# Compression products of a hybrid attention layer: split float32r weights against plain float32 in four column strips

## The chip, the cores and the metric

The kernel runs on one core of a Trainium2 chip. Its time is the device time of one execution in microseconds (us). Before the change it was timed three times, and the median is what a later time is compared with.

## The reference, cut to what matters

One transformer layer over 256 tokens of width 2048, in float32: three attention branches (fox, nsa, dsa), a gated mix, a feed-forward network of width 5632 and a gated extra input. The change touches one piece of the nsa branch: keys and values are compressed. Windows of 32 tokens with a stride of 16 (15 windows) are flattened to 4096 numbers and sent through a two-layer network, once for keys and once for values:

```python
n_cmp = (S - CMP_LEN) // CMP_STRIDE + 1          # 15
tok = c_start[:, None] + jnp.arange(CMP_LEN)[None, :]

def compress(raw, pe, w1, w2):
    blk = (raw[:, tok] + pe).reshape(B, n_cmp, CMP_LEN * dh)   # [15, 32*128]
    return jax.nn.gelu(blk @ w1) @ w2                           # w1 is [4096, 256], w2 is [256, 128]

k_cmp = rope1(compress(kc_raw, pe_k, wk1, wk2), cos[c_end], sin[c_end])
v_cmp = compress(vc_raw, pe_v, wv1, wv2)
```

Only `blk @ w1` is computed in another way after the change. It is 2 x 32 products of a [128 x 15] block with a [128 x 256] piece of `w1`, which is 4 MB for each of the two compressions.

## The kernel before, in words

**Large products.** Nearly all of the time goes to products of the 256 tokens with weight matrices. Each is made of three float32r products: both operands are split into a high and a low half, and high x high, low x high and high x low are summed in PSUM (lines 212 to 214). `weight_group` (line 147) brings one weight tile of 512 KB: a DMA on the queue of SyncE (SP) into `raw` (3 buffers), ScalarE (ACT) rounds it to `whi`, VectorE (DVE) subtracts to get `wlo` (4 buffers each, lines 144 and 145). TensorE (PE) then uses it for 12 products of 512 columns. We call one such tile with its products a stage. A chunk of 512 columns of the input projection has 8 stages, with two accumulators, one for each half of the tokens.

**Side work.** Attention is cut into generators. After every stage `tick()` advances up to three of them, so that their instructions stand between two stages in each engine's program. The tile framework then lays out each engine's instructions by its own plan; the engines work in that order.

**A compression** (`compress`, line 661) is such a generator. `blocks` (line 580) adds the position code to the windows and splits the sum into two halves, side by side in 30 columns. In each of 8 ticks one tile of `w1` (4 of the 32 positions) goes through `weight_group`, with the `raw`, `whi` and `wlo` buffers of the large products, and PE makes 4 x 2 products of 256 columns (lines 670 and 671) with the block as the stationary operand: 30 columns of the array, into 30 rows of one PSUM bank. We call these 8 products a visit; there are 8 visits in a compression, 16 in all. At the end the two halves' rows are summed by a small product with a constant (line 678).

**Neighbours that matter here.** `index_scores` (line 622) makes products for two heads that lie in rows 0 to 63 and 64 to 127 (lines 630 and 631, plain float32). `after_c1` (line 516) normalizes part of the first chunk on DVE (line 530); PE transposes its result at line 537. `queries` and `key_queries` apply rotary tables to a finished chunk with ten DVE instructions (lines 435 to 439), and PE transposes these (lines 446 and 615). `g_tile` (line 342) hands out three buffers of 512 KB, which are used for gates from 330 us on.

Of the kernel before, what the change touches and what calls it, by code (L numbers as in the profile page):

```python
# [10 lines left out]
F32 = mybir.dt.float32  # L11
F32R = mybir.dt.float32r
AF = mybir.ActivationFunctionType
ALU = mybir.AluOpType

P = 128
# [18 lines left out]
NCMP = 15  # L35
# [38 lines left out]
def _const_array():  # L74
    parts, at = [], 0

    def add(name, a):
        nonlocal at
        full = np.zeros((P, a.shape[1]), np.float32)
        full[: a.shape[0]] = a  # L80
        CONST[name] = (at, a.shape[1])
        at += a.shape[1]
        parts.append(full)

    i = np.arange(P)
    causal = np.where(i[None, :] <= i[:, None], 0.0, NEG).astype(np.float32)

    def tables(dim):
        inv = np.float32(1.0) / (np.float32(10000.0) ** (np.arange(0, dim, 2, dtype=np.float32) / np.float32(dim)))
        ang = np.arange(S, dtype=np.float32)[:, None] * inv[None, :].astype(np.float32)  # L90
        return np.cos(ang).astype(np.float32), np.sin(ang).astype(np.float32)

    c, s = tables(HD)
    ci, si = tables(64)
    add("ident", np.eye(P, dtype=np.float32))
    for h in range(2):
        add(f"icos{h}", np.concatenate([ci[h * P:(h + 1) * P]] * 2, 1))
        add(f"isin{h}", si[h * P:(h + 1) * P])
    add("tri", (i[:, None] <= i[None, :]).astype(np.float32))
    CONST["first"] = (0, at)  # L100
    for h in range(2):
        add(f"cos{h}", np.concatenate([c[h * P:(h + 1) * P]] * 2, 1))
        add(f"sin{h}", s[h * P:(h + 1) * P])
    CONST["second"] = (0, at)
    add("mask", np.concatenate([causal, np.zeros((P, P), np.float32), causal], 1))
    ends = np.arange(NCMP) * 16 + 31
    add("cosc", np.concatenate([c[ends]] * 2, 1))
    add("sinc", s[ends])
    ok = (ends[None, :] <= np.arange(S)[:, None]).astype(np.float32)
    for h in range(2):  # L110
        add(f"cmask{h}", np.where(ok[h * P:(h + 1) * P] > 0, 0.0, NEG).astype(np.float32))
    for h in range(2):
        add(f"cok{h}", ok[h * P:(h + 1) * P])
    add("two", np.concatenate([np.eye(NCMP, dtype=np.float32)] * 2, 0))
    return np.concatenate(parts, 1)


# [4 lines left out]
def build(ctx: ExitStack, tc: tile.TileContext, A: dict):  # L122
    nc = tc.nc
    PE, DVE, ACT, POOL = nc.tensor, nc.vector, nc.scalar, nc.gpsimd
# [13 lines left out]
    def sc_tile():  # L138
        return scp.tile([P, 512], F32, name="sc")


    def halves(src, hi, lo):

        ACT.activation(hi, src, AF.Copy)  # L144
        DVE.tensor_sub(lo, src, hi.bitcast(F32))  # L145

    def weight_group(src, nk, w, pool=None):
        raw = wp.tile([P, 1024], F32, name="raw", bufs=3)
        if pool is None:
            hi = wp.tile([P, 1024], F32R, name="whi")  # L150
            lo = wp.tile([P, 1024], F32R, name="wlo")
        else:
            hi, lo = (pool.tile([P, 1024], F32R, name=f"w{x}4", tag="k4") for x in "hl")
        n = nk * w
        nc.sync.dma_start(raw[:, :n].rearrange("p (k w) -> p k w", k=nk), src)
        halves(raw[:, :n], hi[:, :n], lo[:, :n])
        v = lambda t: t[:, :n].rearrange("p (k w) -> p k w", k=nk)
        return v(hi), v(lo)
# [5 lines left out]
    def add(gen, *after):  # L164
        task = {"gen": gen, "after": after, "done": False, "at": 0}
        side.append(task)
        return task
# [174 lines left out]
    def g_tile():  # L342
        return gp.tile([P, 2, 512], F32, name="g", tag="g")
# [10 lines left out]
    with ExitStack() as at:  # L354
        ka = at.enter_context(tc.tile_pool(name="ka", bufs=7))
        cp = at.enter_context(tc.tile_pool(name="cp", bufs=1))
        tm = at.enter_context(tc.tile_pool(name="tm", bufs=2))
# [30 lines left out]
        C = {n: cst[:, a:a + w] for n, (a, w) in CONST.items()}  # L388
        gkv = cp.tile([P, 256], F32, name="gkv")
        fbias = cp.tile([P, 6], F32, name="fbias")  # L390
        peT = cp.tile([P, 2, 32], F32, name="peT")
# [35 lines left out]
        def rope(src, nh, d, cos, sin, out):  # L427

            n = src.shape[0]
            h = d // 2  # L430
            tb = tm.tile([P, 512], F32, name="rb", bufs=1)
            s3 = src.rearrange("p (n d) -> p n d", n=nh)
            o3 = out.rearrange("p (n d) -> p n d", n=nh)
            b3 = tb[:n, :nh * d].rearrange("p (n d) -> p n d", n=nh)
            DVE.tensor_tensor(o3, s3, bc_heads(cos, nh), op=ALU.mult)
            DVE.tensor_tensor(b3[:, :, :h], s3[:, :, h:], bc_heads(sin, nh), op=ALU.mult)
            DVE.tensor_tensor(b3[:, :, h:], s3[:, :, :h], bc_heads(sin, nh), op=ALU.mult)
            DVE.tensor_sub(o3[:, :, :h], o3[:, :, :h], b3[:, :, :h])
            DVE.tensor_add(o3[:, :, h:], o3[:, :, h:], b3[:, :, h:])
# [66 lines left out]
        blk = [None, None]  # L506
        R = {}

        def ra():
            return tm.tile([P, 512], F32, name="ra", bufs=4)  # L510

        def rc():
            return tm.tile([P, P], F32, name="rc")
# [66 lines left out]
        def blocks(j):  # L580

            raw = nsT[:, 2 + j, :]
            win = bass.AP(tensor=raw.tensor, offset=raw.offset, ap=[list(raw.ap[0]), [1, 32], [16, NCMP]])
            a = ra()[:, :32 * NCMP].rearrange("p (l c) -> p l c", l=32)
            DVE.tensor_tensor(a, win, peT[:, j, :].unsqueeze(2).broadcast_to([P, 32, NCMP]), op=ALU.add)
            b = ka.tile([P, 32, 2 * NCMP], F32R, name=f"blk{j}", tag="ka")
            halves(a, b[:, :, :NCMP], b[:, :, NCMP:])
            blk[j] = b


# [69 lines left out]

        def compress(j):
            blocks(j)
            yield
            ph = sc_tile()
            for g in range(8):
                hi, lo = weight_group(A["cmp1"][j, :, g * 4:(g + 1) * 4, :], 4, 256)
                for l in range(4):
                    b = blk[j][:, g * 4 + l, :]
                    first, last = g == 0 and l == 0, g == 7 and l == 3
                    PE.matmul(ph[:2 * NCMP, :256], b, hi[:, l, :], start=first, stop=False)  # L670
                    PE.matmul(ph[:2 * NCMP, :256], b, lo[:, l, :], start=False, stop=last)
                yield
            hid = tm.tile([2 * NCMP, 256], F32, name="hid", bufs=1)
            ACT.copy(hid, ph[:2 * NCMP, :256])
            yield
            pg = sc_tile()
            for n in range(2):
                PE.matmul(pg[:, n * 16:n * 16 + NCMP], hid[:, n * P:(n + 1) * P], C["two"][:2 * NCMP, :],
                          start=True, stop=True)
            x = sm.tile([P, 2, NCMP], F32, name="gx")  # L680
            u = sm.tile([P, 2, NCMP], F32, name="gu")
            DVE.tensor_copy(x, pg[:, :32].rearrange("p (n c) -> p n c", n=2)[:, :, :NCMP])
            DVE.tensor_mul(u, x, x)
            DVE.tensor_mul(u, u, x)
            DVE.scalar_tensor_tensor(u, u, 0.044715, x, op0=ALU.mult, op1=ALU.add)
            ACT.activation(u, u, AF.Tanh, scale=math.sqrt(2.0 / math.pi))
            DVE.tensor_scalar(u, u, 1.0, 0.5, op0=ALU.add, op1=ALU.mult)
            DVE.tensor_mul(u, u, x)
            yield
            pv = sc_tile()  # L690
            for n in range(2):
                PE.matmul(pv[:NCMP, :P], u[:, n, :], cmp2[:, j, n, :], start=(n == 0), stop=(n == 1))
            if j == 1:
                DVE.tensor_copy(cmpv, pv[:NCMP, :P])
                return
            t = rc()
            rope(pv[:NCMP, :P], 1, P, C["cosc"][:NCMP, :], C["sinc"][:NCMP, :], t[:NCMP, :P])
            yield
            tp = sc_tile()
            PE.transpose(tp[:, :NCMP], t[:NCMP, :P], ident[:NCMP, :NCMP])  # L700
            DVE.tensor_copy(cmpk, tp[:, :NCMP])
# [127 lines left out]
    for n in range(4):  # L829
        G = gates(n) if n else G0  # L830
        mix = None
        for name, kt, k0 in (("dsa", 6, 10), ("nsa", 4, 0), ("fox", 6, 4)):
            ps = gemm(A["br_" + name][n], lambda k: O(k0 + k), kt, 512)
            g = G[name]
# [103 lines left out]
    def first_chunk():  # L938
        g = g_tile()
        ps = gemm(A["ffn_in"][0], hT, KT, 512, sizes=[[2] * LONG3], spare=[k4b] * (LONG3 - 4))  # L940
        for h in range(2):
            ACT.activation(g[:, h, :], ps[h], AF.Silu)
        ps = gemm(A["ffn_in"][11], hT, KT, 512)
        for h in range(2):
            DVE.tensor_mul(g[:, h, :], g[:, h, :], ps[h])
        return [g[:, h, :] for h in range(2)]
# [29 lines left out]
    g = first_chunk()  # L976
# [24 lines left out]
    for n in range(4):  # L1001
# [7 lines left out]
        w = 512 // (len(ps) - 1)  # L1009
# [53 lines left out]
```

## Time and profile before

| | us |
|---|---|
| median of three runs | 1613.66 |
| lowest and highest | 1611.16, 1614.71 |
| the profiled execution | 1614.24 |
| its span on the core | 1612.0 |
| PE busy in the span | 1598.5 (99%) |
| DVE busy | 1035.2 (64%) |
| ACT busy | 768.6 (48%) |
| DMA | 198 GB/s over the span |

The span runs from the first to the last instruction of the program. A PE row of the timeline gives the start of a product and the time to its modelled end; since products are pipelined, what one costs is the distance to the next start. `x4` says that four records were merged into one row. PEclk is the granted clock of PE as a share of full speed.

### The profile page before, as it was taken

What the parts mean: (1) busy time and instruction counts of PE and PEld (TensorE: products, weight loads), DVE (VectorE), ACT (ScalarE), POOL (GpSimd) and SP (SyncE); (2) the same over time, 40 slices, a digit from 0 to 9 for tenths busy, and PEclk for the clock granted to TensorE, in tenths of its full rate; (3) what the DMA queues carried; (4) which work ended last, traced back from release to release, by engine and by line L of the source; (5) the groups of instructions that cost most, each with busy time, mean ns of one, the idle gap of its engine ahead of it and who ended that gap; (6) DMA issues with size and microseconds to landing.
All of it is one profiled execution on the core that took longest, in us unless ns stands there. A gap on an engine that the chain in (4) does not pass through costs nothing. (4 is left out here: it accounts for less than half of the span.)

```text
span 1612.0 us, 19950 instructions
## 1 busy us (share of the span) xinstructions
PE 1598.5 (99%) x7521; PEld 1338.9 (83%) x7521; DVE 1035.2 (64%) x1346; ACT 768.6 (48%) x958; POOL 16.9 (1%) x38
## 2 busy tenths in 40 slices
PE   9999999999999999999999999999999999999998
PEld 7777899998888888888888888888888888888787
DVE  5679775554646455465877777787878664545764
ACT  5455554554444444444454444455555453433443
POOL 0000000010000000000000000000000000000000
PEclk9999999999999999999999999999999999999999
DMA  8564654567666666677475565656666776666474
GB/s 266 182 193 148 209 156 117 163 196 237 189 195 186 193 187 193 194 229 222 150 248 170 203 218 200 216 202 222 222 206 223 248 258 194 195 192 199 147 234 132
DMA packets 92752, 319.71 MB, mean 198 GB/s; under 512 B 10608, under 2 KB 11760, under 8 KB 92656
## 3 DMA queue, kind: packets, MB, share of 16 engines
q1 hardware_dynamic: 91376, 314.25, 61.6%
q0 software_dynamic: 1280, 4.20, 0.9%
q8 instruction: 59, 0.97, 0.2%
q14 instruction: 37, 0.30, 0.1%
HBM read 311.58 MB, written 6.82 MB: 198 GB/s over the span
## 5 line engine op out<-in xcount | busy, mean ns | idle before, releaser
L145 DVE TENSOR_TENSOR wlo<-raw,whi 128x1024 fp32r<-128x1024 f32 (+2 forms) x532 | 632.9, 1193 | 498.7 <-ACT whi L144 490.7
L144 ACT ACTIVATE whi<-raw 128x1024 fp32r<-128x1024 f32 (+2 forms) x532 | 549.2, 1035 | 690.1 <-PE acc L213 400.9
L212 PE MATMUL acc<-whi,k4h 128*128 128x512 f32 (+3 forms) x1580 | 608.1, 385 | 1.2 <-ACT k4h L144 0.7
L214 PE MATMUL acc<-wlo,k4h 128*128 128x512 f32 (+3 forms) x1580 | 601.4, 381 | 2.1 <-DVE wlo L145 2.1
L213 PE MATMUL acc<-whi,k4l 128*128 128x512 f32 (+3 forms) x1580 | 602.1, 381 | 0.8 <-DVE k4l L145 0.8
L212 PEld LDWEIGHTS acc<-whi,k4h 128*128 128x128 f32 x1580 | 297.3, 188 | 55.4 <-issue 2.2
L214 PEld LDWEIGHTS acc<-wlo,k4h 128*128 128x128 f32 x1580 | 297.3, 188 | 54.6 <-DVE wlo L145 3.1
L213 PEld LDWEIGHTS acc<-whi,k4l 128*128 128x128 f32 x1580 | 297.6, 188 | 52.1 <-DVE k4l L145 2.0
L257 PE MATMUL sc<-whi,k4h 128*128 128x512 f32 x240 | 94.0, 391 | 0.0
L257 PE MATMUL acc<-whi,k4h 128*128 128x512 f32 x240 | 93.9, 391 | 0.0
L259 PE MATMUL sc<-wlo,k4h 128*128 128x512 f32 x240 | 93.6, 390 | 0.0
L259 PE MATMUL acc<-wlo,k4h 128*128 128x512 f32 x240 | 93.5, 390 | 0.0
L258 PE MATMUL acc<-whi,k4l 128*128 128x512 f32 x240 | 93.5, 390 | 0.0
L258 PE MATMUL sc<-whi,k4l 128*128 128x512 f32 x240 | 93.5, 390 | 0.0
L259 PEld LDWEIGHTS sc<-wlo,k4h 128*128 128x128 f32 x240 | 45.1, 188 | 9.4
L259 PEld LDWEIGHTS acc<-wlo,k4h 128*128 128x128 f32 x240 | 45.1, 188 | 9.4
L258 PEld LDWEIGHTS acc<-whi,k4l 128*128 128x128 f32 x240 | 45.1, 188 | 9.2
L258 PEld LDWEIGHTS sc<-whi,k4l 128*128 128x128 f32 x240 | 45.1, 188 | 9.2
L257 PEld LDWEIGHTS acc<-whi,k4h 128*128 128x128 f32 x240 | 45.1, 188 | 9.2
L257 PEld LDWEIGHTS sc<-whi,k4h 128*128 128x128 f32 x240 | 45.1, 188 | 9.2
L145 DVE TENSOR_TENSOR wtlo<-raw,wthi 128x1024 fp32r<-128x1024 f32 x40 | 48.1, 1223 | 0.0
L144 ACT ACTIVATE wthi<-raw 128x1024 fp32r<-128x1024 f32 x40 | 41.1, 1050 | 1.8 <-DVE raw L282 1.5
(305 smaller groups left out, 1211.9 us busy)
## 6 DMA issues: line engine op xcount, KB each, us to landing
raw<-ffn_in SPq DMA_DIRECT2D x176, 512.0 KB, 4.5
raw<-gate SPq DMA_DIRECT2D x96, 512.0 KB, 3.6
raw<-ffn_out SPq DMA_DIRECT2D x88, 512.0 KB, 4.4
raw<-att_c SPq DMA_DIRECT2D x40, 512.0 KB, 4.4
raw<-att_f SPq DMA_DIRECT2D x48, 384.0 KB, 3.3
raw<-w_out SPq DMA_DIRECT2D x32, 512.0 KB, 4.0
raw<-ple_gate SPq DMA_DIRECT2D x32, 512.0 KB, 4.1
raw<-cmp SPq DMA_DIRECT2D x16, 512.0 KB, 4.4
```

What stands on the lines that cost most here:

```text
L144: ACT.activation(hi, src, AF.Copy)
L145: DVE.tensor_sub(lo, src, hi.bitcast(F32))
L212: PE.matmul(o, xh[:, c], h, start=(k == 0), stop=False)
L213: PE.matmul(o, xl[:, c], h, start=False, stop=False)
L214: PE.matmul(o, xh[:, c], l, start=False, stop=(k == kt - 1))
L257: PE.matmul(o, xh, h, start=first, stop=False)
L258: PE.matmul(o, xl, h, start=False, stop=False)
L259: PE.matmul(o, xh, l, start=False, stop=stop)
```

## The change

The block is no longer split: it is one float32 tile of 32 columns for each position, of which 15 hold windows and 17 are set to zero by GpSimd (POOL). The tiles of `w1` are no longer split either: they are loaded straight into the three `g_tile` buffers and used as they are. A visit now has two tiles: one tick issues their two loads, and the next makes the eight products, each in plain float32 of 256 columns. The four positions of a tile go to four strips of 32 columns of the array (`tile_position=(0, 32 * l)`), and their sums gather in four groups of 32 rows of the PSUM bank. There are 4 visits in a compression, and 8 in all. The constant at the end sums four groups in place of two. A compression still takes 8 ticks for this part.

```diff
-    add("two", np.concatenate([np.eye(NCMP, dtype=np.float32)] * 2, 0))
+    add("four", np.concatenate([np.eye(32, NCMP, dtype=np.float32)] * 4, 0))
...
-            a = ra()[:, :32 * NCMP].rearrange("p (l c) -> p l c", l=32)
-            DVE.tensor_tensor(a, win, peT[:, j, :].unsqueeze(2).broadcast_to([P, 32, NCMP]), op=ALU.add)
-            b = ka.tile([P, 32, 2 * NCMP], F32R, name=f"blk{j}", tag="ka")
-            halves(a, b[:, :, :NCMP], b[:, :, NCMP:])
+            b = ka.tile([P, 32, 32], F32, name=f"blk{j}", tag="ka")
+            POOL.memset(b[:, :, NCMP:], 0.0)
+            DVE.tensor_tensor(b[:, :, :NCMP], win, peT[:, j, :].unsqueeze(2).broadcast_to([P, 32, NCMP]), op=ALU.add)
             blk[j] = b
...
-            for g in range(8):
-                hi, lo = weight_group(A["cmp1"][j, :, g * 4:(g + 1) * 4, :], 4, 256)
-                for l in range(4):
-                    b = blk[j][:, g * 4 + l, :]
-                    first, last = g == 0 and l == 0, g == 7 and l == 3
-                    PE.matmul(ph[:2 * NCMP, :256], b, hi[:, l, :], start=first, stop=False)
-                    PE.matmul(ph[:2 * NCMP, :256], b, lo[:, l, :], start=False, stop=last)
+            for g in range(0, 8, 2):
+                ws = []
+                for i in range(2):
+                    w = g_tile().rearrange("p a (b n) -> p (a b) n", n=256)
+                    nc.sync.dma_start(w, A["cmp1"][j, :, (g + i) * 4:(g + i + 1) * 4, :])
+                    ws.append(w)
                 yield
-            hid = tm.tile([2 * NCMP, 256], F32, name="hid", bufs=1)
-            ACT.copy(hid, ph[:2 * NCMP, :256])
+
+                for i in range(2):
+                    for l in range(4):
+                        PE.matmul(ph[32 * l:32 * (l + 1), :256], blk[j][:, (g + i) * 4 + l, :], ws[i][:, l, :],
+                                  start=(g + i == 0), stop=(g + i == 7), tile_position=(0, 32 * l))
+                yield
+            hid = tm.tile([P, 256], F32, name="hid", bufs=1)
+            ACT.copy(hid, ph[:, :256])
```

The instructions also move against each other, since the framework plans anew. Three places matter. The first is DVE's program at about 37 to 42 us, where the second chunk's weights are split and `after_c1` scales its accumulators (line 530). Before:

```order
L562 SCALAR_TENSOR_TENSOR lf<-lf 128x12
L145 TENSOR_TENSOR wlo<-raw,whi 128x1024 x2
L530 SCALAR_TENSOR_TENSOR ra<-acc,rms,gkv 128x256 x2
L145 TENSOR_TENSOR wlo<-raw,whi 128x1024
L540 COPY nsT<-sc 128x128
```

After:

```order
L562 SCALAR_TENSOR_TENSOR lf<-lf 128x12
L145 TENSOR_TENSOR wlo<-raw,whi 128x1024
L530 SCALAR_TENSOR_TENSOR ra<-acc,rms,gkv 128x256 x2
L145 TENSOR_TENSOR wlo<-raw,whi 128x1024 x2
L540 COPY nsT<-sc 128x128
```

The scaling stands one weight split earlier. On PE the transposes that read it (line 537) stand two products earlier, within the last stage before them.

The second is SP's queue of loads around and after the load of the position code (`peT`, at 46.87 us before); `g` is a tile of `w1`, `raw` a tile of a large product. Before, from the first of its `w1` tiles on, the two kinds took turns in `raw` (`raw<-cmp`, `raw<-att_c`). After:

```order
L668 DMA g<-cmp 128x1024
L405 DMA peT<-peT 128x64
L405 DMA cmp_111<-cmp 128x512
L155 DMA raw<-att_c 128x1024 x15
L668 DMA g<-cmp 128x1024 x2
L155 DMA raw<-att_c 128x1024 x2
L668 DMA g<-cmp 128x1024 x2
L155 DMA raw<-att_c 128x1024 x2
L668 DMA g<-cmp 128x1024
```

The first row is the third `w1` tile; the first two stand after the 13th and the 16th `raw` tile of the program. The fourth to eighth follow in the pattern shown, and each of these waits until PE has used the buffer's former tile. The first visit stands on PE after the 28th stage, the others after the 30th, 32nd and 34th.

The third is DVE's program where the fourth chunk (`acc_820`, `acc_821`) gets its rotary tables, at about 119 to 126 us before. `wlo_1184` is a tile of `w1`, `wlo_1157` and `wlo_1204` are the first two stages of the next chunk. Before:

```order
L145 TENSOR_TENSOR wlo_1157<-raw_1155,whi_1156 128x1024
...
L145 TENSOR_TENSOR wlo_1184<-raw_1182,whi_1183 128x1024
L435 TENSOR_TENSOR ra_1139<-acc_820,cst_106 128x512
...
L439 TENSOR_TENSOR ra_1146<-ra_1146,rb_1147 128x4x64
L645 MATCH_REPLACE work_123<-m8_1173,work_123 128x128
L145 TENSOR_TENSOR wlo_1204<-raw_1202,whi_1203 128x1024
```

After (`wlo_1172` is the third stage of the next chunk, `wlo_1210` the fourth):

```order
L145 TENSOR_TENSOR wlo_1172<-raw_1170,whi_1171 128x1024
...
L644 MATCH_REPLACE work_123<-m8_1113,work_123 128x128
L435 TENSOR_TENSOR ra_1079<-acc_820,cst_106 128x512
...
L439 TENSOR_TENSOR ra_1086<-ra_1086,rb_1087 128x4x64
L643 MAX m8_1113<-work_123 128x8
L145 TENSOR_TENSOR wlo_1210<-raw_1208,whi_1209 128x1024
```

Three stages of the next chunk are now split ahead of the ten rotary instructions, where it was one.

More of the change, by code (lines that the diff above doesn't have):

```diff
@@ L677, in compress @@
             for n in range(2):
-                PE.matmul(pg[:, n * 16:n * 16 + NCMP], hid[:, n * P:(n + 1) * P], C["two"][:2 * NCMP, :],
+                PE.matmul(pg[:, n * 16:n * 16 + NCMP], hid[:, n * P:(n + 1) * P], C["four"],
                           start=True, stop=True)
```

## The prediction

> **What bounds the kernel now.** I read the page first, then the waits of PE, then the timeline around each compression.
>
> ```profile
> span 1612.0 us, 19950 instructions
> PE 1598.5 (99%) x7521; PEld 1338.9 (83%) x7521; DVE 1035.2 (64%) x1346; ACT 768.6 (48%) x958; POOL 16.9 (1%) x38
> ```
>
> PE is the bound: every us of PE time that goes, goes from the end, and work taken from DVE and ACT counts only where PE waits for them. The waits of PE in the first 230 us, which hold both compressions:
>
> ```profile
> PE sc L537 <- DVE ra L530: 2.3, 1, 2.3
> PE acc L214 <- DVE wlo L145: 2.1, 1, 2.1
> PE sc L671 <- DVE wlo L145: 0.9, 1, 0.9
> PE acc L212 <- ACT whi L144: 0.3, 1, 0.3
> PE sc L446 <- DVE ra L439: 0.2, 1, 0.2
> ```
>
> The first two cost more than they show. In the windows view (length, then busy us of PE, PEld, DVE, ACT, POOL, then PEclk, DMA share, GB/s) each is a row of little PE work, and the row behind it has a lower clock:
>
> ```profile
> 38.80:41.50 2.70, 0.39 (x2) 0.00 (x0) 1.65 (x3) 2.02 (x2) 0.00 (x0) 1.00 0.76 255
> 41.50:45.50 4.00, 3.98 (x16) 3.49 (x16) 2.69 (x7) 1.80 (x3) 0.50 (x1) 0.57 0.88 258
> 123.90:126.10 2.20, 0.09 (x1) 0.00 (x0) 2.20 (x7) 0.97 (x2) 0.00 (x0) 1.00 0.06 24
> 126.10:130.60 4.50, 4.47 (x15) 3.64 (x16) 4.33 (x14) 0.82 (x3) 0.00 (x0) 0.62 0.70 208
> 166.60:197.00 30.40, 29.19 (x176) 25.18 (x175) 20.78 (x34) 15.75 (x23) 0.00 (x0) 1.00 0.64 194
> ```
>
> Clock lost: 4.0 x 0.43 and 4.5 x 0.38, 1.7 us each. The last row holds the 0.9 us wait and keeps clock 1.00.
>
> **The products.** The windows view for the block's products alone, one visit each, shows what is removed:
>
> ```profile
> 91.94:92.88 0.94, 0.94 (x8) 0.75 (x8) 0.00 (x0) 0.00 (x0) 1.00 0.70 105
> 95.64:96.57 0.93, 0.93 (x8) 0.75 (x7) 0.00 (x0) 0.00 (x0) 1.00 0.95 374
> 104.93:105.92 0.99, 0.99 (x8) 0.78 (x8) 0.00 (x0) 0.00 (x0) 1.00 0.89 228
> ```
>
> The mean is 0.95 us; 16 visits are 15.2 us.
>
> Plain float32 costs more for a product. Here are two of them on the full array, at their starts:
>
> ```profile
> 146.34 0.38 PE L452 MATMUL sc<-dkT,dq 128*128 128x128 f32 x2
> 146.56 0.60 PE L453 MATMUL sc<-dkT,dq 128*128 128x256 f32 x2
> 147.00 0.38 PE L452 MATMUL sc<-dkT,dq 128*128 128x128 f32 x2
> ```
>
> Each is two records. 128 columns take 0.22 us and 256 take 0.44 (to 147.00), against 0.12 for a float32r product of 256. So 64 products one after another would be 28.2 us. What four strips side by side do, no row shows; the nearest is the index heads, two products in two strips of rows:
>
> ```profile
> 103.75 0.39 PE L214 MATMUL acc<-wlo,k4h 128*128 128x512 f32 x1
> 104.07 0.50 PE L630 MATMUL sc<-dkT,iq 64*128 64x128 f32 x4
> 104.39 0.61 PE L631 MATMUL sc<-dkT,iq 64*128 64x256 f32 x4
> 104.93 0.31 PE L670 MATMUL sc<-whi,blk 128*30 128x256 f32 x1
> 105.07 0.28 PE L671 MATMUL sc<-wlo,blk 128*30 128x256 f32 x1
> 105.19 0.28 PE L670 MATMUL sc<-whi,blk 128*30 128x256 f32 x1
> ```
>
> The four records of line 631 (both heads) take 0.61 us, as the two of line 453 take 0.60: the strips run at the same time. And the program has 630, 631, 630, 631, while all four records of 630 start before 631 does: a strip does not wait for the other's earlier products. The visit also gives the price of going in and out of strips: L214 streams for 0.23 (starts at 103.75), each strip for 0.22 + 0.44, so the work ends at 104.64, and L670 starts at 104.93: 0.29, and 0.02 more in its longer first step.
>
> In the new visit each strip has two products: 2 x 0.44 = 0.88, 0.31 for in and out, some 0.04 for staggered starts: 1.23 us. Eight visits: 9.8. **Products: -5.4 us.** The bounds are 4 at a time and 1 at a time: 8 x (8 x 0.44 + 0.31) = 30.6, which is +15.4. I take 4, because the row-strip rows are the nearest and show full overlap.
>
> [...]
>
> **The wait at 126 us** goes, I think. DVE before:
>
> ```profile
> 119.61 1.21 DVE L145 TENSOR_TENSOR wlo<-raw,whi 128x1024 fp32r<-128x1024 f32 x1
> 120.73 0.68 DVE L435 TENSOR_TENSOR ra<-acc,cst 128x512 f32<-128x512 f32 x1
> ...
> 124.59 0.09 DVE L645 MATCH_VALUE_LOAD work<-m,work 128x8 f32 x1
> 124.66 0.28 DVE L645 MATCH_REPLACE8 work<-m,work 128x128 f32<-128x128 f32 x1
> 124.86 1.22 DVE L145 TENSOR_TENSOR wlo<-raw,whi 128x1024 fp32r<-128x1024 f32 x1
> ```
>
> The ten rotary instructions and the replacement take 4.1 us, and the split that PE needs stands behind them. In the new order three stages of the next chunk are split ahead of them, so from the end of the fourth chunk PE has 3 x 2.75 us (12 products of 0.23), a visit and two rows of transposes, some 10 us; DVE needs 4.1 + 1.3. The extra splits are early enough because `raw` and `whi` no longer serve `w1`: 8 tiles fewer have passed through them by then. PE stood from 123.82 to 126.13: 2.3, and the clock 1.7. **-4.0 us**; bounds 0 and -4.0.
>
> **The wait at 41 us** shrinks. DVE and PE before:
>
> ```profile
> 36.98 1.23 DVE L145 TENSOR_TENSOR wlo<-raw,whi 128x1024 fp32r<-128x1024 f32 x1 [0.91 <-PE acc L213]
> 39.85 1.23 DVE L145 TENSOR_TENSOR wlo<-raw,whi 128x1024 fp32r<-128x1024 f32 x1 [1.64 <-ACT whi L144]
> 40.99 0.87 DVE L530 SCALAR_TENSOR_TENSOR ra<-acc,rms,gkv 128x256 f32<-128x256 f32 x2
> ```
>
> ```profile
> 38.80 0.39 PE L214 MATMUL acc<-wlo,k4h 128*128 128x512 f32 x1
> 41.52 1.69 PE L537 MATMUL sc<-ident,ra 128*128 128x128 f32 x8 [2.33 <-DVE ra L530]
> ```
>
> Line 530 waited behind a split whose tile came late. Now it stands behind the split that ends at 38.21, so line 537 could start at about 38.75 and PE would lose 0.2 instead of 2.5. Against it: the first `w1` load now stands ahead of that split's tile. 512 KB at the 258 GB/s of the row above is 2.0 us, so the delay is 0 to 2.0; I take 1.0. The pause becomes about 1.2 us, nearer to the 0.9 that left the clock at 1.00 than to the 2.5 that did not. **-1.3 and -1.7: -3.0 us**; bounds 0 and -4.0.
>
> **Small waits:** PE's 0.9 at line 671 came from a split of `w1`, which is gone; with the 0.3 and 0.2, and the edges of these waits, **-1.5**.
>
> **The new wait.** The last five tiles of a compression are loaded only when PE has left the buffer, so each has one interval between visits to land in. By the new order these are two stages of 2.75 us, and in the first two an index visit of 0.86 (104.07 to 104.93) for each: 7.2, 7.2 and 5.5 us; in the second compression, with 384-column stages of 2.1, about 5.5, 4.8 and 5.3. Landing takes, from the DMA view:
>
> ```profile
> raw<-cmp SPq DMA_DIRECT2D x16, 512.0 KB, 4.4
> g<-actd SPq DMA_DIRECT2D x9, 512.0 KB, 6.6
> ```
>
> At 4.4 nothing waits; at 6.6 PE loses 0 + 0 + 1.1 + 1.1 + 1.8 + 1.3 = 5.3 us. The nearer row is the first (same source and size): **+1.0 us**. Behind such a load in SP's queue stand `raw` tiles, but six stages are loaded or split ahead when PE leaves a visit (28th stage used, 34th issued), so they have over 10 us.
>
> **At nothing:** the zeroing on POOL (busy 1%) comes long before the first visit; the addition of line 585 stays one instruction, and the halving of the block goes, off PE's path. Should the zeroing hold the first product, it costs its own length once or twice, nearest row 0.5 us for 384 columns:
>
> ```profile
> L624 POOL COPY work<-cst 128x384 f32<-128x384 f32 x1 | 0.5, 503 | 6.2 <-DMA cst<-consts 6.2
> ```
>
> The closing products and the copy of 128 rows for 30 have the same columns.
>
> **Sum:** -5.4 - 4.0 - 3.0 - 1.5 + 1.0 = -12.9 from the profiled 1614.24: 1601.3. The median lies 0.6 lower: 1600.8, say **1601 us**.
>
> **Rivals.**
>
> *One after another.* If float32 products in column strips share what feeds them, the strips give nothing. A visit is 8 x 0.44 + 0.31 = 3.83, the products +15.4; with the waits' -7.5 the time is 1621.5. For it: no row shows column strips, and there all four read different moving tiles over the same rows, unlike the index heads. Against it: the index rows. It decides once a visit exceeds 2.7 us (8 visits then use up the 7.5 of the waits): fewer than 1.5 at a time.
>
> *Strict order.* If a product may start only after all earlier ones have, the two records of one strip stand ahead of the next strip's first: a step of 0.22 for each product, 8 x 0.22 + 0.22 + 0.31 = 2.29 a visit, 18.3 in all: +3.1, and with the waits 1609. The index rows speak against it.
>
> [...]
>
> *Late `w1` tiles.* At 6.6 us: 1605, and 1.7 more for each pause that lowers the clock. For it: visits release one or two loads at once beside `raw` loads.
>
> *The waits stay.* If DVE's new order only moves the stop, the 4.0 and the 3.0 remain: 1608.
>
> **Chances:** forecast 0.55, late tiles 0.13, strict order 0.12, waits stay 0.08, one after another 0.10, else 0.02. No change is within 0.2%, 3.2 us, about what a measurement of this kernel can tell. Faster: 0.55 + 0.13 + 0.08 + half of strict order 0.06 = 0.82; same 0.07; slower 0.11. The forecast's own range is 1597 (both waits fully gone, no new one) to 1605; to hold 8 in 10 it reaches over late tiles, waits that stay and strict order: 1595 to 1612, which leaves out one after another.
>
> **What would show it.** The rows of the new products: 16 records (line 674) within about 1.2 us if four run at a time, 2.3 in strict order, 3.8 one by one. PE waits: L214 <- DVE wlo near 120 us gone, L537 <- DVE ra near 1 us, and the clock at 1.00 from 35 to 200 us. A wait of L674 for DMA would be late tiles. I am wrong if visits exceed 2.7 us, or if a new pause above 2 us comes before 200 us.

## The result, and the profile after

The changed kernel takes **1599.91 us** (median of four runs, 1599.13 to 1600.61) against 1612.5 for the kernel before (four runs beside them, 1611.16 to 1614.71). The ratio is 0.9917, with a 95% interval of 0.9905 to 0.9928: 0.8% faster. The profiled execution took 1599.66 us. The first rows of its page:

```profile
span 1597.9 us, 19880 instructions
PE 1588.7 (99%) x7521; PEld 1327.0 (83%) x7521; DVE 1016.0 (64%) x1328; ACT 752.5 (47%) x940; POOL 18.1 (1%) x40
```

The span is 14.1 us shorter. PE has as many records as before (64 float32 products of two records each replace 128 float32r products of one) and is busy 9.8 us less; the other 4.3 are time in which it stood. The longest waits of PE in the first 230 us (total, times, longest one):

```profile
PE sc L365 <- DVE ones L362: 1.1, 1, 1.1
PE acc L213 <- DVE k4l L145: 0.8, 2, 0.6
PE sc L696 <- DVE gu L692: 0.7, 1, 0.7
PE sc L537 <- DVE ra L530: 0.6, 1, 0.6
```

The 2.1 of line 214 and the 0.9 of line 671 are gone, the 2.3 of line 537 is 0.6, and a wait of line 696 is new. The windows view over the two stretches in which the clock had fallen (length, busy us of PE, PEld, DVE, ACT, POOL, then PEclk, DMA share, GB/s):

```profile
41.50:45.50 4.00, 4.00 (x19) 3.28 (x19) 2.92 (x11) 1.46 (x4) 0.50 (x1) 1.00 1.00 333
120.00:130.60 10.60, 9.94 (x48) 7.84 (x48) 10.29 (x37) 5.71 (x7) 0.00 (x0) 1.00 0.75 230
```

The clock is 1.00 in both. The timeline of PE around one visit (start, time to the modelled end):

```profile
90.97 0.39 PE L214 MATMUL acc<-wlo,k4h 128*128 128x512 f32 x1
91.29 1.07 PE L674 MATMUL sc<-g,blk 128*32 128x256 f32 x16
92.29 0.50 PE L212 MATMUL acc<-whi,k4h 128*128 128x512 f32 x1
```

All 16 records end within 1.07 us, and the next large product starts 1.00 after the first of them. Looked at singly, the first products of the four strips start at 91.291, 91.298, 91.305 and 91.311, 7 ns apart, and the second records from 91.531 on.

How far ahead each place in the program is, told by three pairs of rows (the last two numbers before the forms are the first and the last start). Before:

```profile
L565 PE MATMUL sc<-lf,cst x2: 168/212/255, 55.0 to 55.0; 128*128 128x6 f32 x2
L678 PE MATMUL sc<-cst,hid x8: 257/257/278, 133.4 to 201.0; 30*128 30x15 f32 x8
L335 PE MATMUL sc<-ident,y x64: 269/273/328, 782.6 to 1529.9; 128*128 128x128 f32 x64
```

After:

```profile
L565 PE MATMUL sc<-lf,cst x2: 168/211/254, 51.6 to 51.6; 128*128 128x6 f32 x2
L682 PE MATMUL sc<-cst,hid x8: 177/262/262, 122.7 to 186.0; 128*128 128x15 f32 x8
L335 PE MATMUL sc<-ident,y x64: 270/272/328, 767.5 to 1515.3; 128*128 128x128 f32 x64
```

The kernel is 3.4 us ahead at 55 us, before any product of a compression; 10.7 at the end of the first compression; 15.0 at the end of the second; still 15.1 at 782.6, and 14.6 at 1529.9. Some 0.9 of the 15.0 is given back. 0.4 goes in small steps on PE, nearly all of it before 860 us. The last DVE instruction starts at 1608.71 before and at 1594.10 after, which is still 14.6 apart; the other 0.5 goes behind it, where only the last store and the closing steps are left. Neither was followed further.

### The profile page after: what moved, and what is told of

It is laid out like the page before. It is cut to its first block, busy times and chain, and to the rows that moved or that the text cites. A ratio compares the mean times of both kernels' runs of the same rounds, so it can differ in the third digit from the quotient of the medians.

```text
span 1597.9 us, 19880 instructions
## 1 busy us (share of the span) xinstructions
PE 1588.7 (99%) x7521; PEld 1327.0 (83%) x7521; DVE 1016.0 (64%) x1328; ACT 752.5 (47%) x940; POOL 18.1 (1%) x40
## 5 line engine op out<-in xcount | busy, mean ns | idle before, releaser
L145 DVE TENSOR_TENSOR wlo<-raw,whi 128x1024 fp32r<-128x1024 f32 (+2 forms) x516 | 613.7, 1192 | 502.0 <-ACT whi L144 495.5
L144 ACT ACTIVATE whi<-raw 128x1024 fp32r<-128x1024 f32 (+2 forms) x516 | 533.1, 1036 | 694.0 <-PE acc L213 428.5
L213 PEld LDWEIGHTS acc<-whi,k4l 128*128 128x128 f32 x1580 | 297.2, 188 | 51.6 <-DVE k4l L145 1.5
```

Of the source, the lines that this page charges most:

```text
L213: PE.matmul(o, xl[:, c], h, start=False, stop=False)
```

## The experiments

All edits are against the changed kernel.

### One strip for four

```diff
-                        PE.matmul(ph[32 * l:32 * (l + 1), :256], blk[j][:, (g + i) * 4 + l, :], ws[i][:, l, :],
-                                  start=(g + i == 0), stop=(g + i == 7), tile_position=(0, 32 * l))
+                        PE.matmul(ph[:32, :256], blk[j][:, (g + i) * 4 + l, :], ws[i][:, l, :],
+                                  start=(g + i + l == 0), stop=(g + i + l == 10), tile_position=(0, 0))
```

The closing products and their constant have 32 rows in place of 128.

> The changed kernel with all 64 plain float32 products in the first strip of 32 columns, one sum of 32 rows; loads, buffers and visits as in the changed kernel. Theory (the strips make the gain on PE): the four-strip visits of the changed kernel take 1.10 us from the end of the stream before them, of which 0.88 are products and 0.22 going in and out. In one strip eight products follow each other, 8 x 0.44 + 0.22 = 3.74 us a visit, so 8 x 2.64 = 21.1 us more than the changed kernel's 1599.9: about 1621. The waits at 41 and 126 us should stay small. Rival (the gain comes from plain float32 and the loads, the strips add little): within 3 us of 1600.

Measured: 1621.2 us (1620.22 to 1621.58), ratio to the kernel before 1.0057, interval 1.004 to 1.0074: 0.6% **slower than before**. The timeline of PE around the same visit:

```profile
92.09 0.39 PE L214 MATMUL acc<-wlo,k4h 128*128 128x512 f32 x1
92.41 3.64 PE L674 MATMUL sc<-g,blk 128*32 128x256 f32 x16
95.98 0.50 PE L212 MATMUL acc<-whi,k4h 128*128 128x512 f32 x1
```

From the first product to the next large one it is 3.57 us, which is 8 x 0.446; with the step in, eight visits are 29.5 us. The kernel before spent about 16.0 on its 16 visits counted in the same way (edges to the neighbours included, waits not). So plain float32 by itself costs some 13.5 us here, and it takes the strips to turn that into a gain.

### Two strips for four

```diff
-                        PE.matmul(ph[32 * l:32 * (l + 1), :256], blk[j][:, (g + i) * 4 + l, :], ws[i][:, l, :],
-                                  start=(g + i == 0), stop=(g + i == 7), tile_position=(0, 32 * l))
+                        PE.matmul(ph[32 * (l % 2):32 * (l % 2 + 1), :256], blk[j][:, (g + i) * 4 + l, :], ws[i][:, l, :],
+                                  start=(g + i == 0 and l < 2), stop=(g + i == 7 and l > 1), tile_position=(0, 32 * (l % 2)))
```

The closing products have 64 rows.

> The changed kernel with its products in two strips of 32 columns in place of four. Theory (strips run fully side by side, so time goes with the products in one strip): 4 x 0.44 + 0.22 = 1.98 us a visit in place of 1.10, 7.0 us in all: about 1607. Rival (two strips already feed all that the array takes, or four strips slow each other): a visit near 1.1 us and about 1600.

Measured: 1607.95 us (1606.38 to 1611.06, eight runs), ratio 0.9971, interval 0.9961 to 0.9982. The same visit:

```profile
92.11 1.92 PE L674 MATMUL sc<-g,blk 128*32 128x256 f32 x16
93.96 0.50 PE L212 MATMUL acc<-whi,k4h 128*128 128x512 f32 x1
```

The visit takes 3.57, 1.85 and 1.00 us with one, two and four strips. The steps are 1.72 and 0.85; two strips save four products of 0.44 (1.76), and four save two more (0.88). So the strips overlapped almost in full here (1.72 of 1.76 us and 0.85 of 0.88), and what is left above 8, 4 or 2 products is 0.05, 0.09 and 0.12. The ratio measured for four strips is 3.57 / 1.00 = 3.6, for two 3.57 / 1.85 = 1.9. Three strips were not tried.

### Strip by strip

```diff
-                for i in range(2):
-                    for l in range(4):
+                for l in range(4):
+                    for i in range(2):
```

Both products of a strip now stand behind each other in the program, ahead of the next strip's.

> The changed kernel with the eight products of a visit in another order: both of the first strip, then both of the second, and so on, in place of one in each strip and then again. Theory (each strip works through its own products, whatever stands between them in the program): the 16 records of a visit start within 0.7 us as in the changed kernel, the time within 2 us of it, 1598 to 1602. Rival (products start in program order; the changed kernel only profits from neighbours that lie in different strips): the second strip starts 0.6 us or more behind the first, a visit takes 2 us or more and the time is 7 us or more above, 1607 and up.

Measured: 1600.92 us (one run). The same visit:

```profile
92.01 1.09 PE L674 MATMUL sc<-g,blk 128*32 128x256 f32 x16
93.03 0.50 PE L212 MATMUL acc<-whi,k4h 128*128 128x512 f32 x1
```

It takes 1.02 us for 1.00. In strict order the second, third and fourth strip's first product would each wait until the strip before them had begun its fourth record: three such steps of about 0.66 us (3 records of 0.22) would make 2 us more. They don't: the 16 records take 1.02 us, of which the four on one strip alone take 0.88 (4 x 0.22). That the order on PE did change shows when the records are looked at singly: the four strips start 13 ns apart in place of 7.

### The old loads

```diff
-            for g in range(0, 8, 2):
-                ws = []
-                for i in range(2):
-                    w = g_tile().rearrange("p a (b n) -> p (a b) n", n=256)
-                    nc.sync.dma_start(w, A["cmp1"][j, :, (g + i) * 4:(g + i + 1) * 4, :])
-                    ws.append(w)
-                yield
...
+            for g in range(8):
+                hi, lo = weight_group(A["cmp1"][j, :, g * 4:(g + 1) * 4, :], 4, 256)
+                for l in range(4):
+                    PE.matmul(ph[32 * l:32 * (l + 1), :256], blk[j][:, g * 4 + l, :], hi[:, l, :].bitcast(F32),
+                              start=(g == 0), stop=(g == 7), tile_position=(0, 32 * l))
```

The strips stay, but `w1` goes through `raw`, ACT and DVE again, in 16 visits of one tile. The kernel leaves something out: PE takes only the high half of `w1`, and the low half is split off but not used.

> The new products on the old loads: w1 goes through raw, the rounding and the subtraction as before, 16 visits of one tile, but PE makes one plain float32 product in each of the four strips with the rounded high half. The low half is split and not used, so the result lacks its part. Theory (the products and the waits are two separate gains; the waits go only because w1 leaves raw and the split engines and the plan of DVE changes): visits of 0.44 + 0.22 = 0.66 us, 10.6 in all, some 5 us less than before; PE still waits for the split about 2 us near 41 us and about 2 us near 120 us, each with a lower clock behind it: about 1607. Rival (the waits went because PE is faster in the visits): both waits under 1 us and about 1600.

Measured: 1608.24 us (1607.56 to 1610.45, ten runs), ratio 0.9978, interval 0.9969 to 0.9988. DVE's program has the ten rotary instructions ahead of the next chunk's second split again, and PE has these waits at the two places:

```profile
PE acc L214 <- DVE wlo L145: 1.7, 2, 1.4
PE sc L537 <- DVE ra L530: 1.1, 1, 1.1
```

In the timeline the longer one stands where the kernel before had it:

```profile
124.74 0.50 PE L214 MATMUL acc<-wlo,k4h 128*128 128x512 f32 x1 [1.40 <-DVE wlo L145]
```

and the windows view shows the clock at half behind it:

```profile
122.26:125.67 3.41, 2.01 (x12) 1.56 (x12) 3.41 (x6) 1.39 (x4) 0.00 (x0) 1.00 0.40 101
125.67:129.08 3.41, 3.41 (x10) 2.63 (x9) 3.11 (x15) 1.85 (x2) 0.00 (x0) 0.50 0.86 299
```

So the stop at 126 us comes back with the old loads, though the products stay short: it belongs to the loads and splits of `w1`, with the order of DVE's program that comes with them, and not to the products. It comes back smaller (1.4 for 2.1); why was not looked into. The wait at line 537 is 1.1 and not 2.3, and no half clock follows it: that part was expected about twice as large. The 8.3 us that this kernel is behind the changed one also hold what going in and out of strips 16 times in place of 8 costs (by the 0.2 of one, 1.6), and the parts were not measured singly.

### The first loads later

```diff
                     w = g_tile().rearrange("p a (b n) -> p (a b) n", n=256)
+                    if j == 0 and g + i < 3:
+                        POOL.tensor_copy(w[:1, 0, :1], newest[0].bitcast(F32)[:1, 0, :1])
```

One element is written into each of the first three buffers, from the newest weight tile. A `w1` load now waits until that tile is there.

> The changed kernel with its first three loads of w1 held back until the split of the stage in front of them, as other early loads are held back (three tiny POOL copies). With that the plan puts the scaling of line 530 behind two weight splits again, as before the change; all later places stay as in the changed kernel. Theory (the gain at 41 us comes from that place in DVE's order): PE's wait at line 537 is again above 2 us, the clock halves behind it for about 3.4 us, and the time is 3 to 4 us above the changed kernel's, 1603 to 1604. Rival (the early loads themselves help, or the wait went for another reason): the wait stays near 0.6 us and the time within 1 us of 1600; a second rival is that the first visit now waits for its tiles, which would show as a wait of the new products for DMA.

Measured: 1602.04 us (1600.43 to 1603.81), ratio 0.994, interval 0.9925 to 0.9954: 2.1 above the changed kernel in the median. DVE's order around line 530 is that of before, and the wait is back, while no product of a visit waits for a load:

```profile
PE sc L537 <- DVE ra L530: 2.2, 1, 2.2
```

Line 565 starts at 54.9 us, where the kernel before had 55.0 and the changed one 51.6; so all that had been gained by then is lost again. Not all of these 3.3 us are the wait at line 537, which is 1.6 longer (2.2 for 0.6). PE also waits 1.3 in place of 0.4 for the first rounded inputs, about 9 us from the start (line 212, for ACT's `k4h`; the kernel with the old loads waits 1.3 there too), and 0.6 at line 446. What doesn't come back is the clock that the kernel before lost behind its pause:

```profile
37.64:41.05 3.41, 2.50 (x12) 1.73 (x10) 1.64 (x2) 1.27 (x2) 0.17 (x1) 1.00 0.74 244
41.05:44.46 3.41, 2.15 (x14) 1.97 (x15) 3.41 (x8) 1.80 (x3) 0.00 (x0) 1.00 0.92 301
44.46:47.87 3.41, 3.26 (x15) 2.36 (x13) 1.92 (x6) 1.06 (x1) 0.80 (x3) 1.00 0.63 222
```

The pause (2.34 us from the end of the stream ahead, for 2.49 before) is nearly as long, and the clock stays at 1.00. The wait is set by DVE's order, as the prediction had it; the 1.7 us of clock did not come with this pause, though they came with one of 2.49. The section on the hardware returns to this.

### The `raw` buffers for the `w1` tiles

```diff
-                    w = g_tile().rearrange("p a (b n) -> p (a b) n", n=256)
+                    w = wp.tile([P, 1024], F32, name="raw", bufs=3).rearrange("p (a n) -> p a n", n=256)
```

Everything else of the change stays, but the tiles share the three buffers of the large products' loads.

> The changed kernel with the unsplit w1 tiles in the three raw buffers of the large products in place of gate tiles. Theory (separate buffers are needed, since PE holds an unsplit tile until its visit while a split one is free after the split): a raw tile behind the visit is loaded only when PE frees a buffer, and needs 4.4 us to land, 1.06 to be rounded and 1.22 to be subtracted, 6.7 us in all, against a stage of 2.75 and sometimes an index visit of 0.86: PE waits about 3 us for each of the 8 visits, and the clock halves behind most of them (1.7 us): about 1630, between 1615 and 1645. Rival (the gate tiles are no part of the gain): 1600 to 1603.

Measured: 1615.99 us (one run, beside 1613.55 for the kernel before). The longest waits of PE from 80 to 200 us:

```profile
PE acc L212 <- ACT whi L144: 4.2, 5, 1.7
PE sc L704 <- DVE rc L439: 1.3, 1, 1.3
PE acc L214 <- DVE wlo L145: 1.0, 3, 0.4
```

Direction as expected, size not: some 15 us above the changed kernel and not the 30 that stood as the likely value. While a `w1` tile sits in `raw` until its visit, only one or two buffers are left for the large products, and PE waits for ACT's rounding of tiles that land late. Two things that were expected did not come: a wait of about 3 us for each visit (the five of the first row are 4.2 together), and half clock behind them (it is 1.00 up to the end of the program). The framework's plan broke one visit up (its pieces stand at 99.76, 101.44 and 104.07, with 2, 8 and 6 records); whether this kept the loss small is not shown. The waits listed are 6.5 of the 15 us, and the rest was not followed. Without the free `g_tile` buffers nothing of the gain is left.

### Pauses made on purpose

The half clock was worth 3.4 us of the kernel before, so three kernels put pauses of graded length into the part from 330 us on, where PE otherwise hardly stops (0.6 us in all, by its waits there): a chain of copies on DVE from a finished accumulator, on which a small product ahead of the next gate chunk waits.

```diff
+    def pause(ps, n):
+        src = last_ps[0][1][:, :64]
+        t = keep.tile([P, 64], F32, name="pz")
+        DVE.tensor_copy(t, src)
+        for _ in range(3 * n):
+            DVE.tensor_copy(t, t)
+        for o in ps:
+            PE.matmul(o[:, :64], ident, t, start=True, stop=True)
```

> The changed kernel with nine pauses of PE of growing length in the gate products of the second to fourth column block: each of these nine products starts only when a chain of small DVE copies, 1, 4, 7 up to 25 of them one after another, has read the product before it and come back through a tiny product. What is looked at is the granted clock behind each pause. Theory (a pause of PE of some 2 us or more halves the clock for 3.4 us, a shorter one does not): the pauses up to about 1 us leave the clock at 1.00, those above 2.3 us are followed by a half clock, and the switch lies between 0.9 and 2.3. Rival (what counts is something else at the two places, such as narrow products after the pause): no half clock behind any of the nine, or no relation to their length. The time is longer by the pauses, which tells nothing else.

Measured: 1653.9 us (one run). Only six of the nine chains held PE up, and these pauses came out longer than meant, at 3.2, 4.0, 5.2, 6.0, 7.3 and 8.1 us. Behind each of them the clock is at half. So the expected switch between 0.9 and 2.3 us could not be seen here. The windows view around the first:

```profile
440.12:443.53 3.41, 0.41 (x3) 0.06 (x1) 1.95 (x5) 1.54 (x2) 0.00 (x0) 1.00 0.51 159
443.53:446.94 3.41, 3.41 (x10) 2.92 (x11) 0.00 (x0) 0.00 (x0) 0.00 (x0) 0.50 0.54 154
```

The two kernels with shorter chains read the other accumulator (`last_ps[0][0]`), and make `n` and `8 - n` copies behind the first:

> The changed kernel with pauses as in the run of nine pauses, but shorter: the chain starts from the half of the product before that ends 1.4 us earlier, and has 2 to 9 copies of about 0.25 us. Six of the nine were real pauses there; here these should be about 1.3 to 3.1 us long, in steps of 0.25 or 0.5. Theory (the clock is set for fixed slices of 3.41 us, by how busy PE was in the slice before; the runs so far halve it behind 2.01 us busy and not behind 2.15): a pause is followed by a half clock only where it leaves a whole slice with about 2 us of PE or less, so that pauses below 1.3 us never do it, those above 2.8 us always, and between them the place of the pause against the slices decides. Rival (the length of the pause decides by itself): one length parts the halved from the others, with no exception.

> The same with the lengths in falling order, so that the same lengths meet the slices at other places. Theory (fixed slices): a length between 1.3 and 2.8 us that halves the clock in one of the two runs can fail to in the other. Rival (length alone): each length does the same in both.

Measured, one run each: 1613.69 and 1609.18 us. The first has pauses of 0.70, 0.92 and 1.38 us without a half clock, and one of 2.98 with it. Its windows around the 1.38 (first two rows) and around the 2.98:

```profile
621.82:625.23 3.41, 2.21 (x13) 1.57 (x12) 2.51 (x9) 1.54 (x2) 0.00 (x0) 1.00 0.55 167
625.23:628.64 3.41, 3.41 (x17) 2.80 (x16) 0.77 (x1) 1.06 (x1) 0.00 (x0) 1.00 0.51 154
645.71:649.12 3.41, 0.60 (x5) 0.31 (x3) 2.57 (x9) 1.54 (x2) 0.00 (x0) 1.00 0.53 160
649.13:652.54 3.41, 3.41 (x11) 2.75 (x10) 0.00 (x0) 0.00 (x0) 0.00 (x0) 0.50 0.49 154
```

The second has 0.46, 0.69, 1.15 and 1.38, none with a half clock. No pause between 1.4 and 2.9 us came about, and just there the theory of length and the theory of fixed slices would differ; by themselves these three kernels don't decide between them.

## Why the prediction was right, point by point

Forecast 1601 us, measured 1599.91; the sum was -12.9 from the profiled execution, and the profiled executions differ by 14.6 (1614.24 to 1599.66).

**Four at a time: right.** The row strips of the index heads were the nearest row, and the column strips overlapped as fully: 1.00 us a visit, of which the two products of one strip are 0.88. The two rivals against it fell by experiment: one strip alone costs 3.57 us a visit (the prediction had put one after another at 3.83), and the strict order's 2.29 is neither in the changed kernel (1.00) nor in the one whose program is written strip by strip (1.02). (The prediction has 2.7 us a visit as the length from which the strips would have cost more than the waits give back; by its own terms it is 2.8, the eighth part of 15.2 + 7.5. Nothing hung on it.)

**The products: -5.4 predicted, some -6.4 to -7 measured.** This is the term that was mis-sized. A visit was put at 0.88 + 0.31 + 0.04 = 1.23. Counted from the end of the stream ahead to the next large product, visits measure 1.09 to 1.19, and the eight sum to 8.97: going in takes 0.10 (0.20 where an index visit stands ahead) and leaving 0.09, for which the prediction took the index visit's 0.31; the stagger is 0.02, not 0.04. And the visits of before were priced by their windows (0.95 each, 15.2), which leave out part of the edge to the neighbours; counted like the new ones they are about 16.0.

**The wait at 126 us: -4.0 predicted, -4.0 measured.** Line 214 has no wait for the split left, and the clock is 1.00 from 120 to 130.6. The places say the same: between lines 565 and 678 the lead grew from 3.4 to 10.7, by 7.3, which is about 4.0 and four visits of 0.8. That the loads and splits of `w1` caused it, the kernel with the old loads shows, where 1.4 of the 2.1 comes back.

**The wait at 41 us: -3.0 predicted, -3.4 measured** (line 565). The scaling stands where the order showed it, between two splits:

```profile
37.55 1.23 DVE L145 TENSOR_TENSOR wlo<-raw,whi 128x1024 fp32r<-128x1024 f32 x1 [1.66 <-ACT whi L144]
38.69 0.87 DVE L530 SCALAR_TENSOR_TENSOR ra<-acc,rms,gkv 128x256 f32<-128x256 f32 x2
39.48 2.59 DVE L145 TENSOR_TENSOR wlo<-raw,whi 128x1024 fp32r<-128x1024 f32 x2
```

The split ahead of it ends at 38.78. The prediction had 38.21 if nothing held it, and up to 2.0 more because a `w1` load stands ahead of its tile; it took 1.0, and it was 0.6. The pause on PE is 0.82 for the 1.2 foreseen. In three kernels with the same first loads the wait of 0.6 is longer (0.9 with one strip, 1.0 strip by strip, 1.2 with two strips), so 0.6 lies at the low end of what this order gives. And 0.2 to 0.3 of the 3.4 are there before the scaling, since PE waits 0.4 for the first rounded inputs and the kernel before 0.7. The kernel with late first loads gives the wait back with the order, so the cause of the wait is shown. The other half of the term, 1.7 of clock that goes with the pause, came true here but did not come in that kernel, where the clock behind a pause of 2.34 us stayed at 1.00.

**The small waits: -1.5 predicted, about -1.9 measured.** Line 671's wait is gone with its edges (1.07 us on PE), and the 0.3 of line 212 and some 0.5 of edges with it.

**The new wait: +1.0 predicted, none measured.** The view of loads:

```profile
g<-cmp SPq DMA_DIRECT2D x16, 512.0 KB, 4.6
```

Single loads took 3.6 to 6.7 us. The tightest was issued at 167.59 and landed at 171.57, for a visit at 172.99. The prediction gave each of the last five tiles of a compression one interval between visits to land in. By the three buffers this holds for three of them, with which its sum was made; the other two are needed one visit later. The nearer of the two rows that the prediction had (4.4) was the right one.

**Not foreseen: +0.8.** In its place PE waits at line 696, where the second layer of the first compression starts. Its input is DVE's, and DVE's timeline shows what stands between the pieces of it:

```profile
128.71 0.42 DVE L643 MAX8 m<-work 128x8 f32<-128x256 f32 x1
129.04 0.16 DVE L691 TENSOR_SCALAR gu<-gu 128x30 f32<-128x30 f32 x1
129.16 0.09 DVE L644 MATCH_VALUE_LOAD work<-m,work 128x8 f32 x1
129.24 0.41 DVE L644 MATCH_REPLACE8 work<-m,work 128x256 f32<-128x256 f32 x1
129.56 0.18 DVE L692 TENSOR_TENSOR gu<-gu,gx 128x30 f32<-128x30 f32 x1
```

The two small steps of the activation are interleaved with the selection's maximum and replacement (lines 643 and 644), which the new order brought here:

```profile
129.89 0.60 PE L696 MATMUL sc<-cmp,gu 128*15 128x128 f32 x4 [0.66 <-DVE gu L692]
```

**At nothing: right.** POOL sets the 17 columns of each block to zero far ahead of the first visit:

```profile
L585 POOL MEMSET blk<- 128x544 f32 x2 | 1.2, 580 | 62.1 <-PE sc L630 62.1
```

That is 2 x 0.58 us, and PE waits for none of it. The addition behind it takes 0.99 to 1.01 us, as before.

**The sum of what was measured**: -6.8 for the products (the middle of the two counts), -4.0, -3.4, -1.9 and +0.8 are -15.3; the lead at line 682's last start is 15.0. With the 0.9 given back later it is -14.1 for the span. That the prediction hit within 1.1 us is luck in part: it has errors of one sign (the products 1.4, the wait that didn't come 1.0, the waits at 41 us and the small ones 0.8) and of the other (the wait at line 696 0.8, what was given back later 0.9), 3.2 against 1.7.

## What to carry to other kernels

Plain float32 was a loss as long as it ran product by product (+13.5 us here), and a gain only because, with a stationary operand of 32 columns, four products ran side by side in four column strips (1.00 us a visit for 3.57 in one); ask for the strips before giving up split operands. More than half of the gain, however, came from the engines around PE: once the tiles no longer pass through the shared buffers, the rounding and the subtraction, two waits shrink or go that had nothing to do with the products themselves (2.3 to 0.6 us at line 537, 2.1 to none at line 214). What the clock adds to such a wait was not the same in every run, as the next section shows. So read, in a change that frees a shared buffer, what the order of the other work becomes on the engine that fed it, and give the new loads buffers of their own (in the shared buffers the same change gained nothing: 1615.99 beside 1613.55, one run each).

## What the runs showed of the hardware

**Half clock came in stretches of 3.41 us, on one grid in each run.** Pauses are counted here from the end of the stream ahead, which makes them 0.1 to 0.3 us longer than the idle time in the rows. Their length doesn't sort them: 2.49 and 2.31 us were followed by half clock (the kernel before), 1.66 too (the old loads), but 2.34 was not (late first loads), and neither was 1.80 (the `raw` buffers). What sorts nearly all of them is where they fall. The half-clock stretches found inside the programs are 3.41 us long or a whole multiple of it, and within one run they begin on one grid. In the kernel with the long pauses they begin at 443.53, 470.83, 545.93, 576.65, 651.74 and 682.46: 8, 30, 39, 61 and 70 times 3.413 us behind the first, within 0.02. In the kernel before, the windows cut on that grid:

```profile
38.46:41.87 3.41, 1.08 (x7) 0.62 (x6) 2.02 (x4) 2.11 (x2) 0.00 (x0) 1.00 0.76 262
41.87:45.28 3.41, 3.41 (x13) 2.95 (x12) 2.10 (x6) 1.80 (x3) 0.50 (x1) 0.50 0.87 243
123.79:127.20 3.41, 1.27 (x6) 0.89 (x6) 3.41 (x8) 1.79 (x3) 0.00 (x0) 1.00 0.14 28
127.20:130.61 3.41, 3.41 (x12) 2.75 (x11) 3.24 (x13) 0.00 (x0) 0.00 (x0) 0.50 0.83 265
```

The two stretches begin 25 x 3.4133 apart, and the clock falls once more at 1612.00, after the last product, 460 x 3.4133 behind the first: in this run one grid held to the end. The slices with PE busy for 1.08 and 1.27 of their 3.41 us were each followed by a slice at half clock, which cost about 1.7. The grid of the run with late first loads shows only at its end, where the clock falls at 1600.94, after the last product; 457 x 3.4133 before that is 41.05, inside the pause of 2.34 us (an estimate, which takes the 3.4133 from the kernel before). By it the pause was cut in two, its slices kept 2.50 and 2.15 us of work, and nothing followed.

The share of work from which the clock is kept is not settled. Slices with 2.15 and 2.21 kept it and those with 1.27 and less lost it; but one with 2.01 lost it (the old loads) and one with 2.00, at 38 us in the kernel with pauses of 0.70 to 2.98, did not:

```profile
38.14:41.55 3.41, 2.00 (x14) 1.46 (x13) 2.52 (x4) 1.86 (x2) 0.17 (x1) 1.00 0.80 293
```

Further off is the pause of 1.80 us with the `raw` buffers. Its slice, on the grid counted back from 1614.10, where the clock of that run falls at the end, has 1.68 and kept the clock:

```profile
173.68:177.09 3.41, 1.68 (x20) 0.86 (x20) 0.67 (x1) 1.06 (x1) 0.00 (x0) 1.00 0.73 226
177.09:180.50 3.41, 3.10 (x13) 1.91 (x11) 1.68 (x2) 1.06 (x1) 0.00 (x0) 1.00 0.93 322
```

Most of its work is a visit, 16 records four at a time; whether these count for more was not tested. Ends of products are modelled, so these figures are not exact either, and what parts the slices between 1.3 and 2.1 stays open. The span began at another place of the grid in each run: counted back by 3.4133, the first boundary is at 0.91 us in the profiled run before, at 2.79 with the old loads, 3.21 and 0.60 in two of the runs with pauses and 0.09 with late first loads. The same pause could then cost 1.7 us in one execution and nothing in the next; this is the author's inference, since each kernel has one profiled execution. The kernel before, with two pauses of over 2 us, ranged from 1611.05 to 1615.93 in 17 runs, and the changed one, with none, from 1599.13 to 1600.61 in four. The mean granted clock of each of the 17 runs points the same way: the three with 0.997 or 0.998 took 1613.30 to 1615.93, the fourteen with 0.999 or 1.000 took 1611.05 to 1614.57. With late first loads it is less clear (1602.57 at 1.000, 1600.43 at 0.999), so the clock is at most one reason among others.

**Four column strips ran side by side.** 16 records in four strips took 1.00 us in one order of the program and 1.02 in the other, where one strip's share alone is 0.88 (2 products of 0.44) and all of them in one strip took 3.57; going in and out cost about 0.2 (0.10 and 0.09). Split float32r products in column strips were not tried.
